# A fixed order for the prologue of a two-block transformer kernel: norm weight spread by a product, first weight chunk loaded ahead of the second token tile

## The chip, the core and the metric

The kernel runs on one core of a Trainium2 chip. The metric is the device time of one execution in microseconds (us). Before the change three runs gave 1746.03, 1747.23 and 1747.4 us; the median is 1747.23.

Engines in the profile: PE is TensorE's matmul, PEld its weight load, DVE is VectorE, ACT is ScalarE, POOL is GpSimd, and SP is SyncE, whose queue (SPq) issues every DMA of this kernel in order.

## The reference, cut to what matters

The input `x` has 256 tokens of width 1024. The first step is a norm and one wide projection; all that follows (dilated attention, retention, memory attention, a mixture of experts, and a second block of two layers) needs it.

```
def rms_norm(x, w, eps=1e-6):
    y = x * rsqrt(mean(x * x, axis=-1) + eps)
    return y * w

x = x + parallel_mixer(rms_norm(x, norm_mix_w), w_in, ...)   # proj = h @ w_in, cut into q, k, v, rq, rk, rv, rg
x = x + memory_cross_attention(...)
x = x + hierarchical_moe(...)        # 32 experts, 200 MB of weights
# second block: two layers of ffn, four mixers, ffn
```

Everything is float32. A dense product is made of three: each operand is split into a high part in the float32r type (`xh`, `wh`) and the low remainder (`xl`, `wl`), and high x high, high x low and low x high are added up in PSUM.

## The kernel before, in words

The tokens are two tiles of 128 (t = 0, 1). The width of 1024 is eight blocks of 128 (k = 0 to 7). A dense weight is packed in chunks of 1 MB; for a projection of 512 columns a chunk holds four k blocks, and `weight` (L265) cuts it into two parts of two k blocks. For each part ACT writes `wh` (L279, a copy with rounding) and DVE or POOL writes `wl` (L283, raw minus `wh`). The buffers `wh` and `wl` have three slots (`wsp`), so part n+3 can be converted only when the products of part n are done for both token tiles. The ring of raw chunks has four buffers.

Which engine writes `wl` is set by two lists: the first two parts of the kernel go to POOL (`on_pool = [None, None]`, L203), and of the others every fourth by a running count (`nw`, `pool_mod = 4`, L206, L282). From the second block's mixers on, `pool_mod` is 0.

`mixer1` (L522) is the prologue. It clears a tile, multiplies it with itself WARM = 18 times on PE (L531, work that nobody reads), loads `x` tile 0 in two halves, `ident`, `x` tile 1, the norm weight as a broadcast to 128 partitions (L238, 512 KB written), and the first weight chunk in two halves (L260). For each token tile ACT squares and sums (L1003), DVE and POOL form 1/rms (L416, L418: POOL's `pow`), DVE multiplies by it and by the norm weight (L508), PE transposes four blocks at a time (L401), ACT and DVE split the result into `xh` and `xl` (L391, L392). Then `dilated` (L569) projects K, Q and V by `dense_nat` (L314); K's, with `stagger=True`, is the first dense product of the kernel: 48 products of 128 x 512 in four parts.

Who goes first: the tile framework takes the instructions in program order as priority and arranges each engine's queue with a planner that models times; only where `manual_schedule` names an engine does the written order hold on it. An engine runs its queue strictly in order. So an instruction may stand in front of another that was written earlier. SPq, too, is arranged by the planner. `issue_after` ties one instruction behind another on the same engine.

`retention_start` (L608) opens the buffers of the retention, loads `ret_gn_w` as a broadcast (L238) and computes `log_decay` (L639), 23 small DVE instructions one after another with one exponential on ACT; its result is used by the retention, about 100 us later. It also clears four pieces of `rqp` on POOL (L558).

Much later the weights of the experts (`mraw`, L823) stream through buffers that the memory attention gives up one by one; L968 consumes them.

## Time and profile before

| | |
|---|---|
| Median of three runs | 1747.23 us |
| Profiled execution, its own device time | 1748.11 us |
| Its span in the trace | 1746.5 us |
| PE busy | 1582.8 us, 91% of the span |
| DVE, ACT, POOL busy | 48%, 38%, 16% |
| Chain that ended last | PE 54%, DMA 21%, DVE 3%, issue 2%, POOL 1%, ACT 1% |
| DMA | 419.07 MB, mean 240 GB/s |

The chain that ended last is followed back from the last instruction: at each step to what released it. A busy PE is not PE at its peak, since a product at the lower granted clock counts as busy as well. A wait for several semaphores is put down to the one that came last.

### The profile page before, as it was taken

How to read it: one execution, taken by the hardware profiler on the slowest of the kernel's cores; microseconds unless marked ns; L12 is line 12 of the kernel's file. 1: busy time of each engine (PE TensorE's matmuls, PEld its weight loads, DVE VectorE, ACT ScalarE, POOL GpSimd, SP SyncE). 2: the span in 40 equal slices, each digit the busy share in tenths (PEclk: the TensorE clock that was granted, in tenths of full speed). 3: DMA queues.
4: the chain of work that ended last, by engine and by line, in shares of the span. 5: the costliest groups of instructions: out<-in, count | busy, mean ns of one | idle time of the engine just before them, and what ended most of it. 6: DMA issues, size and time to landing. Idle time of an engine off the chain costs nothing.

```text
span 1746.5 us, 24953 instructions
## 1 busy us (share of the span) xinstructions
PE 1582.8 (91%) x10070; PEld 1217.7 (70%) x10070; DVE 839.2 (48%) x1468; ACT 657.5 (38%) x1125; POOL 286.5 (16%) x253
## 2 busy tenths in 40 slices
PE   8999898877767776899999989999999999989998
PEld 6777774322211221699988769999999988779997
DVE  5657653000000000454577675556655667765555
ACT  4655441000000000444445745444444536734442
POOL 4223321100000000222233250000100041340000
PEclk9999998888878777999999989999999999989999
DMA  8444859999999999855553235556455634155551
GB/s 273 143 178 158 319 192 421 417 421 421 420 420 421 421 420 421 346 180 186 196 180 126 96 145 181 185 190 241 145 194 181 247 110 141 49 185 187 178 190 73
DMA packets 66188, 419.07 MB, mean 240 GB/s; under 512 B 10642, under 2 KB 12178, under 8 KB 18706
## 3 DMA queue, kind: packets, MB, share of 16 engines
q1 hardware_dynamic: 66064, 417.39, 63.1%
q8 instruction: 82, 1.34, 0.3%
q14 instruction: 42, 0.33, 0.1%
HBM read 416.32 MB, written 1.05 MB: 239 GB/s over the span
## 4 chain that ended last, share of the span: by engine, by line
PE 54%; DMA 21%; DVE 3%; issue 2%; POOL 1%; ACT 1%; DVEq 0%; SPq 0%; POOLq 0%; ACTq 0%
DMA mraw<-in_wm 21%; PE ps L310 17%; PE ps L312 17%; PE ps L311 17%; PE ps L401 1%; PE ps L480 1%; DVE xa L1211 1%; PE ps L968 0%; PE ps L945 0%; POOL rq L418 0%; DVE wl L283 0%; DVE xl L392 0%; DVE lnst L1239 0%; POOL ropet L1423 0%; DMA raw<-in_wd 0%
## 5 line engine op out<-in xcount | busy, mean ns | idle before, releaser
L283 DVE TENSOR_TENSOR wl<-raw,wh 128x1024 fp32r<-128x1024 f32 (+2 forms) x314 | 389.5, 1251 | 300.8 <-ACT wh L279 298.2
L279 ACT ACTIVATE wh<-raw 128x1024 fp32r<-128x1024 f32 (+2 forms) x356 | 370.9, 1052 | 349.7 <-PE ps L311 179.9
L310 PE MATMUL ps<-xh,wh 128*128 128x256 f32 x1424 | 402.1, 282 | 3.4 <-ACT cv L1511 3.4
L312 PE MATMUL ps<-xh,wl 128*128 128x256 f32 x1424 | 401.4, 282 | 0.0
L311 PE MATMUL ps<-xl,wh 128*128 128x256 f32 x1424 | 401.0, 282 | 0.0
L310 PEld LDWEIGHTS ps<-xh,wh 128*128 128x128 f32 x1424 | 268.3, 188 | 6.6 <-ACT cv L1511 3.8
L311 PEld LDWEIGHTS ps<-xl,wh 128*128 128x128 f32 x1424 | 268.4, 188 | 1.4
L312 PEld LDWEIGHTS ps<-xh,wl 128*128 128x128 f32 x1424 | 268.4, 188 | 0.8
L968 PE MATMUL ps<-mraw,xg 128*32 128x512 f32 x1024 | 171.4, 774 | 69.1 <-DMA mraw<-in_wm 68.9
L312 PE MATMUL ps<-wh,xl 128*128 128x512 f32 (+3 forms) x520 | 190.0, 370 | 7.4 <-DVE xl L392 7.2
L310 PE MATMUL ps<-wh,xh 128*128 128x512 f32 (+3 forms) x520 | 190.3, 375 | 4.8 <-ACT xh L391 4.1
L311 PE MATMUL ps<-wl,xh 128*128 128x512 f32 (+3 forms) x520 | 191.6, 369 | 2.7 <-POOL wl L283 1.3
L968 PEld LDWEIGHTS ps<-mraw,xg 128*32 128x32 f32 x1024 | 26.5, 120 | 201.5 <-DMA mraw<-in_wm 166.1
L418 POOL TENSOR_TENSOR rq<-rv,mhalf 128x1 f32<-128x1 f32 (+4 forms) x46 | 46.9, 1020 | 729.0 <-DVE rv L416 726.3
L283 POOL TENSOR_TENSOR wl<-raw,wh 128x1024 fp32r<-128x1024 f32 x42 | 103.6, 2472 | 280.9 <-ACT wh L279 182.0
L974 DVE TENSOR_TENSOR mf<-ps,mf 128x512 f32<-128x512 f32 x8 | 5.5, 692 | 238.1 <-PE ps L968 234.1
L312 PEld LDWEIGHTS ps<-wh,xl 128*128 128x128 f32 x520 | 100.6, 194 | 24.0 <-DVE xl L392 11.2
L310 PEld LDWEIGHTS ps<-wh,xh 128*128 128x128 f32 x520 | 100.6, 194 | 22.7 <-ACT xh L391 7.5
L311 PEld LDWEIGHTS ps<-wl,xh 128*128 128x128 f32 x520 | 101.0, 194 | 18.4 <-POOL wl L283 3.4
L311 PE MATMUL ps<-wl,hf 128*128 128x512 f32 x256 | 100.1, 391 | 0.0
L312 PE MATMUL ps<-wh,hf 128*128 128x512 f32 x256 | 100.1, 391 | 0.0
L310 PE MATMUL ps<-wh,hf 128*128 128x512 f32 x256 | 98.2, 390 | 0.0
(355 smaller groups left out, 1980.1 us busy)
## 6 DMA issues: line engine op xcount, KB each, us to landing
mraw<-in_wm SPq DMA_DIRECT2D x191, 1024.0 KB, 19.8
raw<-in_wd SPq DMA_DIRECT2D x179, 1024.0 KB, 4.9
raw<-in_wd SPq DMA_DIRECT2D x8, 512.0 KB, 10.9
raw<-in_wd SPq DMA_DIRECT2D x4, 832.0 KB, 4.3
bc_ln_g<-in_ln_g SPq DMA_DIRECT2D x6, 512.0 KB, 5.8
bc_ln_b<-in_ln_b SPq DMA_DIRECT2D x6, 512.0 KB, 6.6
raw<-in_wd SPq DMA_DIRECT2D x4, 768.0 KB, 4.2
bias<-in_bias SPq DMA_DIRECT2D x4, 512.0 KB, 5.8
```

The source lines that it names most:

```text
L279: s.nc.scalar.activation(h[:, :n], rc, AF.Copy)
L283: i = eng.tensor_tensor(l[:, :n], rc, h[:, :n].bitcast(F32), op=OP.subtract)
L310: mm(out, lhsT=lh, rhs=rh, start=start, stop=False)
L311: mm(out, lhsT=lh, rhs=rl, start=False, stop=False)
L312: mm(out, lhsT=ll, rhs=rh, start=False, stop=stop)
L401: s.nc.tensor.transpose(ps[:, b * 128:b * 128 + 128], src[:, b * 128:b * 128 + 128], s.ident)
L418: s.last_pow = s.nc.gpsimd.tensor_tensor(q, r, s.mhalf[:, :n], op=OP.pow)
L480: s.nc.tensor.matmul(out, lhsT=v(j), rhs=pt[:, 2 * i + j], start=first and j == 0, stop=last and j == 1)
L968: nc.tensor.matmul(ps[32 * e:32 * e + 32], lhsT=xg[:, k, 32 * e:32 * e + 32], rhs=w[:, e * FF:e * FF + FF], start=k == 0, stop=k == NK - 1 ...
L974: nc.vector.tensor_tensor(f, gu[1], f, op=OP.mult)
L1211: nc.vector.scalar_tensor_tensor(z[:, cs], z[:, cs], mv[:, 0:1], g[:, cs], op0=OP.subtract, op1=OP.mult)
```

## The change

- `mixer1` calls a new function `norm1`. The norm weight is loaded as one row of 4 KB and put on all partitions by two PE products with a row of ones (K = 1, float32), into the two PSUM banks "b". DVE's multiplications read it there.
- WARM is 14 instead of 18; the two products stand behind the tenth.
- SPq's written order is: first half of `x` tile 0, the row, second half, `ident`, the first chunk in two halves, `x` tile 1.
- On PE, ACT and DVE the prologue has a written order: tile 0 through its norm, the first chunk's conversion (both `wl` on DVE), 12 products of tile 0 with the first chunk, then tile 1 through its norm.
- `on_pool` is empty and `nw` starts at -4; the first chunk's parts aren't counted. So the parts that go to POOL are, in the order of the parts, numbers 6, 10, 14, ... instead of 1, 2, 4, 8, 12, ...
- `retention_start` stands before the products and no longer loads `ret_gn_w` or computes `log_decay`; both come after `dilated`, and `log_decay`'s first DVE instruction is tied behind the last `wl` that DVE had been given until then.

```
-WARM = 18
+WARM = 14
-        s.on_pool = [None, None]
+        s.on_pool = []
-        s.nw, s.pool_mod = 0, 4
+        s.nw, s.pool_mod = -4, 4
     def dense_nat(s, x, n, done, stagger=False, first=None):
+        if first:
+            w[0] = first(ps[0])
         if stagger:
             for t in range(NT):
-                for c in range(2):
+                for c in range(1 if first and not t else 0, 2):
                     part(t, c)
     def mixer1(s):
...
-            wn = s.bcast(p, "norm_mix_w", D)
-            s.ahead = [s.raw(cuts=2)]
-            for t in range(NT):
-                for c, z in s.rms(p, x[t], wn):
-                    s.tsplit(hs, t, z[:, c * 512:], k0=4 * c, n=4)
-        o = s.xsplit()
...
+            with ExitStack() as c1:
+                first = s.norm1(s.pool(c1, "rms1", side="right"), x, hs)
+                r = s.retention_start(ctx)
+                o = s.xsplit()
+                with ExitStack() as c2:
+                    s.dilated(c2, hs, o, first)
+            r["gnw"] = s.bcast(r["p"], "ret_gn_w", 512)
+            r["lg"] = s.log_decay(r["p"])
+    def norm1(s, p, x, hs):
+        nc = s.nc
+        halves = [slice(c * 512, c * 512 + 512) for c in range(2)]
+        warm = p.tile([128, 512], F32R, name="warm")
+        nc.vector.memset(warm.bitcast(F32), 0.0)
+        one = p.tile([1, 128], F32, name="one")
+        nc.vector.memset(one, 1.0)
+        row = p.tile([1, D], F32, name="row")
+        for c, cs in enumerate(halves):
+            nc.sync.dma_start(x[0][:, cs], s.a["x"][:128, cs])
+            if not c:
+                nc.sync.dma_start(row, s.a["norm_mix_w"])
+        nc.sync.dma_start(s.ident, s.a["ident"])
+        raw = s.raw(cuts=2)
+        nc.sync.dma_start(x[1], s.a["x"][128:])
+        z = [p.tile([128, D], F32, name=f"z{t}") for t in range(NT)]
+        ps, wn = s.bank("mm"), [s.bank("b") for _ in range(2)]
+        w = [[s.wsp.tile([128, CH // 2], F32R, name=n, tag=n) for n in ("wh", "wl")] for _ in range(2)]
+        part = [raw[:, i * 1024:i * 1024 + 1024] for i in range(2)]
+        hi = lambda i: nc.scalar.activation(w[i][0], part[i], AF.Copy)
+        lo = lambda i: nc.vector.tensor_tensor(w[i][1], part[i], w[i][0].bitcast(F32), op=OP.subtract)
+        def tile(t, between):
+            q = s.rms_scale(z[t], x[t])
+            for c, cs in enumerate(halves):
+                nc.vector.scalar_tensor_tensor(z[t][:, cs], x[t][:, cs], q, wn[c], op0=OP.mult, op1=OP.mult)
+            tp = [s.transpose4(z[t][:, cs]).rearrange("p (b c) -> p b c", b=4) for cs in halves]
+            tk = slice(t * 128, t * 128 + 128)
+            between()
+            for c in range(2):
+                nc.scalar.activation(hs[0][:, 4 * c:4 * c + 4, tk], tp[c], AF.Copy)
+            for c in range(2):
+                h = hs[0][:, 4 * c:4 * c + 4, tk]
+                nc.vector.tensor_tensor(hs[1][:, 4 * c:4 * c + 4, tk], tp[c], h.bitcast(F32), op=OP.subtract)
+        order = s.tc.manual_schedule(engines={mybir.EngineType.PE, mybir.EngineType.Activation, mybir.EngineType.DVE})
+        def first(out):
+            with order:
+                for i in range(WARM):
+                    if i == WARM - 4:
+                        for c, cs in enumerate(halves):
+                            nc.tensor.matmul(wn[c], lhsT=one, rhs=row[:, cs], start=True, stop=True)
+                    nc.tensor.matmul(ps, lhsT=warm[:, :128], rhs=warm, start=True, stop=True)
+                tile(0, lambda: hi(0))
+                hi(1)
+                lo(0)
+                lo(1)
+                for a, b in ((0, 0), (1, 0), (0, 1)):
+                    for k in range(4):
+                        cs = slice(k % 2 * 512, k % 2 * 512 + 512)
+                        nc.tensor.matmul(out, lhsT=hs[a][:, k, :128], rhs=w[k // 2][b][:, cs], start=a + b + k == 0,
+                                         stop=False)
+                tile(1, lambda: None)
+            return w
+        return first
     def log_decay(s, p):
-        nc.vector.scalar_tensor_tensor(na, d, -1.0, d, op0=OP.mult, op1=OP.min)
+        s.issue_after(nc.vector.scalar_tensor_tensor(na, d, -1.0, d, op0=OP.mult, op1=OP.min), s.last_lo)
```

## Rows read from the trace of the kernel before

**Rows 1.** Stretches: length, busy PE PEld DVE ACT POOL, granted clock, DMA share, GB/s.
```profile
25.00:50.00 25.00, 24.31 (x112) 19.73 (x110) 19.50 (x48) 11.48 (x17) 9.85 (x8) 1.00 0.56 187
260.00:264.00 4.00, 4.00 (x19) 3.34 (x18) 1.38 (x2) 0.00 (x0) 0.00 (x0) 1.00 1.01 424
360.00:710.00 350.00, 252.49 (x1412) 61.72 (x1411) 22.52 (x54) 14.93 (x25) 17.76 (x23) 0.79 1.01 420
```

**Rows 2.** SP's timeline (start, length in us) and its waits (total, times, longest).
```profile
250.89 9.72 SPq L823 DMA_DIRECT2D mraw<-in_wm  x9
...
SPq L823 <- POOL wl L283: 13.0, 1, 13.0
```

**Rows 3.** PE's timeline of the prologue: start, length, instruction, idle before and releaser.
```profile
1.60 6.62 PE L531 MATMUL ps<-warm 128*128 128x512 f32 x18 [1.60 <-DVE warm L528]
11.11 1.32 PE L401 MATMUL ps<-ident,rms 128*128 128x128 f32 x8 [2.89 <-DVE rms L508]
...
15.32 0.80 PE L311 MATMUL ps<-wl,xh 128*128 128x512 f32 x1 [0.41 <-POOL wl L283]
16.33 0.63 PE L310 MATMUL ps<-wh,xh 128*128 128x512 f32 x1
16.76 0.63 PE L311 MATMUL ps<-wl,xh 128*128 128x512 f32 x1
20.84 0.39 PE L310 MATMUL ps<-wh,xh 128*128 128x512 f32 x1
21.07 0.40 PE L311 MATMUL ps<-wl,xh 128*128 128x512 f32 x1
```

**Rows 4.** Half-microsecond stretches of PE: length, busy, granted clock, DMA share, GB/s.
```profile
13.00:13.50 0.50, 0.43 (x1) 0.75 0.99 378
...
20.00:20.50 0.50, 0.50 (x3) 0.92 1.03 418
...
225.50:226.00 0.50, 0.00 (x0) 1.00 0.12 49
...
228.00:228.50 0.50, 0.50 (x4) 0.79 1.00 426
```

**Rows 5.** ACT's timeline of the prologue and the K projection.
```profile
8.50 0.63 ACT L1003 ACTIVATE rms<-x 128x512 f32<-128x512 f32 x1 [3.46 <-DMA x<-in_x]
11.47 1.06 ACT L279 ACTIVATE wh<-raw 128x1024 fp32r<-128x1024 f32 x1 [1.64 <-DMA raw<-in_wd]
12.43 0.58 ACT L391 ACTIVATE xh<-ps 128x512 fp32r<-128x512 f32 x1
21.10 1.06 ACT L279 ACTIVATE wh<-raw 128x1024 fp32r<-128x1024 f32 x1 [0.51 <-PE ps L312]
29.04 1.06 ACT L279 ACTIVATE wh<-raw 128x1024 fp32r<-128x1024 f32 x1 [0.58 <-PE ps L312]
```

**Rows 6.** DVE's timeline of the prologue, and one instruction of `log_decay`.
```profile
10.31 2.74 DVE L508 SCALAR_TENSOR_TENSOR rms<-x,rq,bc_norm_mix_w 128x512 f32<-128x512 f32 x4 [0.23 <-DMA bc_norm_mix_w<-in_norm_mix_w]
13.04 0.69 DVE L392 TENSOR_TENSOR xl<-ps,xh 128x512 fp32r<-128x512 f32 x1
30.13 1.23 DVE L283 TENSOR_TENSOR wl<-raw,wh 128x1024 fp32r<-128x1024 f32 x1 [0.73 <-ACT wh L279]
36.15 0.17 DVE L659 TENSOR_TENSOR lsacc<-lsacc,lsw 128x8 f32<-128x8 f32 x1
```

**Rows 7.** POOL's timeline of the prologue.
```profile
5.37 0.55 POOL L418 TENSOR_TENSOR rq<-rv,mhalf 128x1 f32<-128x1 f32 x1 [3.98 <-DVE rv L416]
12.60 4.99 POOL L283 TENSOR_TENSOR wl<-raw,wh 128x1024 fp32r<-128x1024 f32 x2 [1.89 <-ACT wh L279]
```

**Rows 8.** The chain that ended last: start, length, what.
```profile
463.94 3.60 PE ps L994 x4
```

**Rows 9.** PE's waits from 20 to 110 us: total, times, longest.
```profile
PE ps L311 <- POOL wl L283: 0.9, 1, 0.9
PE ps L401 <- DVE lsacc L661: 0.7, 1, 0.7
```

## The prediction

> **What bounds the kernel now.** I read the page's shares first, then the stretches, then the timelines of the first 30 us engine by engine. From 25 us on PE is busy 24.31 of 25 us at the full clock [rows 1]: behind the prologue the K, Q and V projections are one dense stream of products. The experts are bound by the DMA: from about 260 to 710 us it moves 420 GB/s at a share of 1.0 [rows 1]. That stream begins with nine loads that SP issues from 250.89 us [rows 2], into buffers which the memory attention frees as PE goes on. So an earlier start of PE's dense stream passes through to the end one for one, if nothing between reorders: what is to be sized is the start.

> In the prologue PE's warm-up ends at 8.22; it idles 2.89 us until DVE has multiplied by the broadcast norm weight (10.31, released by that weight's DMA), transposes, and waits at 15.32 for the first chunk's low part from POOL [rows 3, 6]. POOL needs 4.99 us for two such parts [rows 7], DVE 1.23 for one [rows 6]. The granted clock falls to half at about 13.25 and comes back at about 20.0 [rows 4]; meanwhile products start 0.43 us apart (16.33, 16.76), afterwards 0.23 (20.84, 21.07) [rows 3]. A slot of `wh` is free when both tiles have used it: the fourth part is converted at 21.10, the seventh, which needs the end of K's last part, at 29.04 [rows 5]. So **K's 48 products end at 29.0 us**; that is the mark which I recompute.

> **The change, part by part.** Landing times I take by position in SP's queue. Before, the third block of 512 KB (`x` tile 1) was there at 8.50, the next (the broadcast) at 10.31, the next (first half of the chunk) at 11.47 [rows 5, 6]. After, these places are taken by the chunk's halves and then `x` tile 1, with one more small load in front, whose issue I estimate at 0.4 us: first half 8.9, second 10.7, tile 1 11.9. If the broadcast was itself slow they come up to 1.5 us earlier; the chain below wins at most 0.5 by it, since ACT then does its steps in the same order.

> Warm-up: ten products 0.43 apart end at 1.60 + 4.4 = 6.0. The two float32 products of 512 columns I price by four of the same width that take 3.60 us, 0.9 each [rows 8]; theirs have 128 rows and these one, so each may cost from 0.23 (a product of one pass at full clock) to 1.8 (half clock). I take 0.9, the same type and width: 7.8, and four warm products at 0.23 end at 8.7. The four dropped ones cost nothing, as nobody reads them. 1/rms of tile 0 is ready at 5.37 + 0.55 [rows 7], plus 0.4 for the later second half: 6.3; the first product at 6.9 ends later. DVE multiplies (2.74/4 = 0.69 each [rows 6]) until 7.7 and 8.5; eight transposes take 1.32 [rows 3]: 8.7 to 10.0. Nothing waits on the price of the two products unless it passes about 1.2 each.

> ACT in the written order: first `wh` (1.06 [rows 5]) 8.9 to 10.0, two `xh` (0.58 each) to 11.2, second `wh` to 12.25. DVE: `xl` (0.69 [rows 6]) 10.6 to 11.3 and to 12.0, the two `wl` (1.23) to 13.25 and 14.5. PE: high x high for k0 and k1 at 10.6, the rest from 12.25, the last products with `wl` 14.5 to 15.0: twelve products done. Taking `wl` from POOL thus costs DVE 2.5 us which tile 1 waits for: its two small DVE steps stand behind (14.9), POOL's `pow` 0.55 (15.5), two multiplications (16.25, 16.95), transposes to 17.65, first `xh` at 17.6. Meanwhile only the third slot is free, so PE can do six products of tile 0 on k4 and k5, four of them surely. From 17.65 thirty products remain, 30 x 0.23 = 6.9: **K ends at 24.5, 4.5 us earlier.** Bounds: 24.0 if the chunk lands early; 25.1 if the planner puts the third `wl` on DVE into `pow`'s gap (0.6 later); 26.0 if ACT and DVE convert nothing of the second chunk before tile 1 is through (third `wh` at 18.25, its `wl` done at 20.55, twenty-four products after that). So 3.0 to 5.0.

> Next, the later stages. PE's waits between 20 and 110 us that this touches are 0.9 on a `wl` of POOL and 0.7 behind `log_decay` on DVE [rows 9]. The `wl` parts of POOL move from the second chunk of each projection to the first, and `log_decay` behind the last `wl` of V; so both waits may go (1.6 gained), or come back in another place: `log_decay` is 23 instructions of about 0.2 us from start to start (0.17 busy [rows 6]), 4.6 us of chain on DVE in the dilated attention. I take a gain of 0.5, the range is -4.6 to +1.6. The loads of `ret_gn_w` and of the decays leave SP's queue at 20 us; behind them stood raw chunks that have a ring of four ahead, so I cost that at nothing; without that cover it is about 0.4 each, three of them. Clearing `rqp` on POOL, four instructions, falls where POOL now has no `wl`: nothing. The banks "b" are free at 17, and Q needs them at 24.5: nothing; if not, Q's start would wait.

> Sum: 4.5 + 0.5 = 5.0 us. The profiled execution took 1748.11 around a span of 1746.5, 0.9 above the median 1747.23; the difference applies to either, so **1742.2 us** against the median.

> **Rivals.** *The clock falls again.* It fell at 13.25 after the idle 2.89 us and a run of transposes, and at about 228.2 after a shorter gap (PE idle from 225.5 to 226.0) and a few products [rows 3, 4]. After the change PE has transposes from 8.7, two products, a gap of 1.1 us, and a gap before tile 1. Against it: no gap is as long as the first. If it falls at 13 and stays low until 20, transposes end 0.7 later, four more products remain undone or run at 0.43 instead of 0.23, and K ends near 26.4: gain 2.6 + 0.5 = 3.1, **1744.1**. [...]

> *The moved chain costs what the prologue gives.* `log_decay`'s 4.6 us on DVE stand in front of the softmax: 4.5 - 4.6, about zero, **1747.3**. For it: PE already waited once behind that chain [rows 9]. Against: it is split over short instructions among which the planner puts others.

> *Slower: the experts' stream starts later.* Place: SP's queue before 250.89. SP once stood 13.0 us in front of an `mraw` load, held by a `wl` on POOL [rows 2]. The count that chooses POOL's parts is shifted, so the part that holds SP may now be one in front of the nine loads. If they wait 13.0 more, the stream, which has no slack until 710, ends 13.0 - 5.0 = 8.0 us later than before: **1755.2**. It decides from 5.0 us of wait on. Against: those loads also follow PE, which is early.

> *Chances.* A measurement tells 0.2%, 3.5 us, from no change. Forecast, with 1738 to 1743.7 as its own range (gains of 3.5 to 9, the larger if both later waits go and the planner's new order helps): 0.52. Clock: 0.20; moved chain and the closed order of the second chunk: 0.16, all within 0.2%. Later stream: 0.12. So faster 0.52, same 0.36, slower 0.12. The range 1736 to 1750 holds the first three with a later re-planning of a few us either way, and leaves out the late stream.

> **What would show it.** Right: the norm's multiplication at about 7.0 with PSUM as its operand; the first dense product near 10.6; twelve done by 15.0; tile 1's first `xh` near 17; the seventh `wh` conversion at 24.5 instead of 29.04; a clock of 1.0 from 6 us on; the nine `mraw` loads at about 246. Wrong: half clock between 13 and 20; `xh` of tile 1 after 18.5; PE waiting behind `lsacc` after 50 us; or the 420 GB/s stretch beginning no earlier than before although K ends early.

## The result, and the profile after

The changed kernel takes 1759.27 us (median of five runs, 1755.08 to 1761.74) against 1746.96 for the kernel before beside it: a ratio of 1.0068, 95% interval 1.0057 to 1.0079. It is **12 us slower**; 1742.2 was forecast, with 1736 to 1750 as the range. The profiled execution took 1757.29 us around a span of 1755.6, 9.2 more than the profiled one of before.

The stretches of [rows 1], after:

```profile
25.00:50.00 25.00, 24.23 (x102) 18.88 (x101) 14.83 (x21) 11.72 (x15) 10.78 (x6) 0.93 0.52 173
260.00:264.00 4.00, 4.00 (x20) 3.39 (x19) 2.43 (x6) 1.15 (x3) 0.00 (x0) 1.00 0.92 295
```

The clock has a dent in the dense stream (0.93 instead of 1.00), and at 260 us the experts' loads are not yet at full rate (295 GB/s instead of 424). The loads themselves, answering to [rows 2]:

```profile
14.81 0.43 SPq L694 DMA_DIRECT2D decay<-in_ret_decay_b  x1
...
197.65 2.48 SPq L872 DMA_DIRECT2D mraw<-in_wm  x5
253.90 10.12 SPq L872 DMA_DIRECT2D mraw<-in_wm  x7
```

The first `mraw` load leaves SP at 197.65; before it left at 191.51. So two thirds of the profiled loss arise before 200 us. The loads that [rows 2] show from 250.89 start at 253.90. PE's timeline of the prologue, answering to [rows 3]:

```profile
5.82 1.98 PE L593 MATMUL ps<-row,one 1*128 1x512 f32 x4
...
10.50 1.22 PE L602 MATMUL ps<-wh,xh 128*128 128x512 f32 x2
17.66 1.29 PE L406 MATMUL ps<-ident,z 128*128 128x128 f32 x8 [0.35 <-DVE z L577]
24.33 0.50 PE L314 MATMUL ps<-wh,xl 128*128 128x512 f32 x1 [1.61 <-DVE xl L585]
...
28.04 0.63 PE L312 MATMUL ps<-wh,xh 128*128 128x512 f32 x1
28.46 0.63 PE L313 MATMUL ps<-wl,xh 128*128 128x512 f32 x1
```

Down to the first dense product this is the forecast: the two row products in 1.98 us, the first dense product at 10.50 (forecast 10.6). Then PE stands 1.61 us for an `xl` of tile 1, and soon afterwards, from 25.65 to 28.9, products start 0.42 to 0.43 apart instead of 0.23, at a granted clock of 0.50 from 26 to 29. What held that `xl` is seen on DVE, whose columns are those of [rows 6]:

```profile
18.96 0.69 DVE L585 TENSOR_TENSOR xl<-ps,xh 128x512 fp32r<-128x512 f32 x1 [0.79 <-ACT xh L582]
23.51 0.17 DVE L712 TENSOR_SCALAR lg<-decay 128x8 f32<-128x8 f32 x1 [3.87 <-DMA decay<-in_ret_decay_b]
23.59 0.68 DVE L585 TENSOR_TENSOR xl<-ps,xh 128x512 fp32r<-128x512 f32 x1
```

Between the two `xl` the planner has put `lg`, a step of 8 columns of `log_decay` that needs only the decays (min(decay, 0)). The change ties only `na`, the chain's other first step, behind V. The decays' DMA, issued at 14.81, landed 8.6 us later, and DVE stood for it 3.87 us, with the second `xl` behind it, whose `xh` ACT had ended at 19.59. On ACT and POOL, answering to [rows 5, 7], the lambdas do the same:

```profile
24.44 0.21 ACT L1239 ACTIVATE ls<-ls 128x2 f32<-128x2 f32 x1 [4.86 <-DVE ls L1238]
24.55 2.94 ACT L279 ACTIVATE wh<-raw 128x1024 fp32r<-128x1024 f32 x3
...
30.69 1.06 ACT L279 ACTIVATE wh<-raw 128x1024 fp32r<-128x1024 f32 x1 [0.60 <-PE ps L314]
```

```profile
14.97 0.89 POOL L639 TENSOR_TENSOR qk<-col_attn_q_norm_w,col_attn_k_norm_w 128x1 f32<-128x1 f32 x1 [7.20 <-DMA col_attn_k_norm_w<-in_attn_k_norm_w]
16.15 0.58 POOL L423 TENSOR_TENSOR rq<-rv,mhalf 128x1 f32<-128x1 f32 x1
23.67 0.32 POOL L1236 TENSOR_TENSOR lm<-bc_diff_lambda 128x64 f32<-128x64 f32 x1 [6.95 <-DMA bc_diff_lambda<-in_diff_lambda]
```

ACT's exponential of the lambdas (`ls`) stands 4.86 us ahead of three `wh` conversions, so the fourth of K comes at 24.55 instead of 21.10, and the seventh, the mark of K's end, at 30.69. Before it was 29.04; the forecast was 24.5. POOL's `qk` holds tile 1's `pow` (`rq`) until 16.15, and `lm` has POOL stand for 6.95 us. Later PE waits, answering to [rows 9] (total, times, longest):

```profile
PE ps L312 <- DVE rqp L400: 2.3, 1, 2.3
PE ps L314 <- DVE xl L585: 1.6, 1, 1.6
```

The first of these ends at 64.33, and the granted clock is 0.50 from 64 to 70. One more wait lies far behind, at the start of the second block, behind a low part for which DVE needs 2.74 us, instead of about 1.2, beside one of POOL:

```profile
724.65 0.39 PE L313 MATMUL ps<-wl,xh 128*128 128x256 f32 x1 [2.30 <-DVE wl L283]
```

```profile
721.86 2.74 DVE L283 TENSOR_TENSOR wl<-raw,wh 128x1024 fp32r<-128x1024 f32 x1
...
721.15 2.36 POOL L283 TENSOR_TENSOR wl<-raw,wh 128x1024 fp32r<-128x1024 f32 x1 [77.78 <-DVE x L966]
```

### The profile page after: what moved, and what is told of

Read it like the earlier page. It is cut to its first block, busy times and chain, and to the rows that moved or that the text cites. A ratio compares the mean times of both kernels' runs of the same rounds, so it can differ in the third digit from the quotient of the medians.

```text
span 1755.6 us, 24956 instructions
## 1 busy us (share of the span) xinstructions
PE 1591.8 (91%) x10070; PEld 1221.3 (70%) x10070; DVE 840.9 (48%) x1471; ACT 659.0 (38%) x1125; POOL 281.6 (16%) x251
## 4 chain that ended last, share of the span: by engine, by line
PE 65%; DMA 24%; DVE 5%; issue 2%; POOL 2%; ACT 1%; SPq 0%; DVEq 0%; ACTq 0%; POOLq 0%
DMA mraw<-in_wm 23%; PE ps L312 20%; PE ps L314 19%; PE ps L313 19%; PE ps L406 2%; PE ps L485 2%; PE ps L1017 1%; DVE xa L1260 1%; POOL rq L423 1%; DVE wl L283 1%; PE ps L994 1%; DMA col_attn_q_norm_w<-in_attn_q_norm_w 1%; DMA decay<-in_ret_decay_b 0%; ACT wh L279 0%; DVE dtmp L757 0%
## 5 line engine op out<-in xcount | busy, mean ns | idle before, releaser
L283 DVE TENSOR_TENSOR wl<-raw,wh 128x1024 fp32r<-128x1024 f32 (+2 forms) x313 | 383.2, 1234 | 296.9 <-ACT wh L279 295.8
L1017 PE MATMUL ps<-mraw,xg 128*32 128x512 f32 x1024 | 175.4, 789 | 67.4 <-DMA mraw<-in_wm 67.2
L283 POOL TENSOR_TENSOR wl<-raw,wh 128x1024 fp32r<-128x1024 f32 x41 | 99.9, 2441 | 338.7 <-ACT wh L279 229.2
```

What stands on the lines that cost most here:

```text
L283: i = eng.tensor_tensor(l[:, :n], rc, h[:, :n].bitcast(F32), op=OP.subtract)
L1017: nc.tensor.matmul(ps[32 * e:32 * e + 32], lhsT=xg[:, k, 32 * e:32 * e + 32], rhs=w[:, e * FF:e * FF + FF], start=k == 0, stop=k == NK - 1 ...
```

## The experiments

Two theories stood at first. **A**: small steps with late operands, in front of tile 1's work on in-order engines, cost most of the 12 us. **D**: the shifted count, by which GpSimd gets other low parts, costs most of it. The table has every run's result. The ratio is to the kernel before, measured beside it; it is not the quotient of the two medians, so the two can differ. The marks are from one profiled execution of each kernel: the seventh `wh` conversion (K's end), the first product with `pt` and `va` (dilated attention), the first `mraw` load, and the span less that load (all that comes later).

| kernel | median us | ratio [95%] | 7th wh | first pt,va | first mraw | rest |
|---|---|---|---|---|---|---|
| before | 1747.0 to 1747.7 | | 29.04 | 74.20 | 191.51 | 1555.0 |
| changed | 1759.27 | 1.0068 [1.0057, 1.0079] | 30.69 | 80.11 | 197.65 | 1558.0 |
| before_pool_count | 1758.93 | 1.0063 [1.0049, 1.0077] | 28.87 | 83.47 | 201.34 | 1558.0 |
| before_chain_moved | 1747.80 | 1.0004 [0.9994, 1.0013] | 28.62 | 74.03 | 191.16 | 1554.7 |
| tie_small_steps | 1754.18 | 1.0039 [1.0026, 1.0053] | 26.68 | 75.05 | 194.41 | 1558.1 |
| pool_count | 1750.38 | 1.0017 [1.0008, 1.0026] | 30.61 | 77.11 | 194.56 | 1555.0 |
| both_and_late_chain | 1754.70 | 1.0045 [1.0031, 1.0058] | 29.87 | 74.70 | 195.89 | 1554.7 |
| ties_and_count | 1753.37 | 1.0026 [1.0015, 1.0036] | 33.09 | 79.90 | 197.35 | 1555.5 |
| chain_as_before | 1754.45 | 1.0040 [1.0026, 1.0053] | 32.39 | 81.19 | 198.13 | 1554.7 |
| chain_after_ret_proj | 1753.45 | 1.0037 [1.0023, 1.0050] | 29.99 | 73.78 | 193.76 | 1554.9 |
| pool_ties | 1746.02 | 0.9992 [0.9983, 1.0001] | 29.75 | 74.91 | 193.44 | 1554.2 |
| k_parts_on_dve | 1743.80 | 0.9991 [0.9981, 1.0001] | 26.08 | 69.90 | 188.31 | 1550.4 |
| full_row_product | 1744.55 | 0.9984 [0.9975, 0.9993] | 27.45 | 71.29 | 190.94 | 1555.0 |
| chain_at_q | 1746.35 | 0.9995 [0.9986, 1.0004] | 26.34 | 72.33 | 190.72 | 1553.6 |
| v_part_on_dve | 1748.31 | 1.0003 [0.9994, 1.0012] | 25.19 | 74.75 | 188.61 | 1553.4 |
| v_part_and_chain_at_q | 1746.40 | 0.9997 [0.9988, 1.0006] | 25.94 | 75.58 | 189.52 | 1553.7 |

The profiled execution is not always near its kernel's median: that of k_parts_on_dve took 1740.40 us (its other ten 1743.27 to 1749.15), that of v_part_on_dve 1743.68, of full_row_product 1747.55 and of pool_ties 1749.27. Differences of a microsecond or two between the marks of two kernels mean little.

**before_pool_count**: the kernel before, with the shift of the count alone.

```
-        s.nw, s.pool_mod = 0, 4
+        s.nw, s.pool_mod = -2, 4
```

> The kernel before with only the count that picks GpSimd's low parts shifted, to where the changed kernel has it from the second chunk on; the first two parts stay on GpSimd. Theory A: the prologue stays (seventh wh at about 29.0, as the first chunk's parts are where they were); the wait on GpSimd's low part in the projections goes or moves (within 1 us); FFN 0 starts 1.5 to 2.7 us later; together 1 to 3 us slower than before (ratio 1.0005 to 1.002). Rival D: the shift costs most of the loss by itself, 8 to 12 us (ratio 1.005 to 1.007).

Measured +11.5 us. Theory D holds, against what I expected: the shift alone costs as much as the whole change. One stretch of the kernel before, and then those of this run (columns as in [rows 1]):

```profile
60.00:62.00 2.00, 2.00 (x20) 2.00 (x18) 0.71 (x2) 0.73 (x2) 2.00 (x1) 1.00 0.00 0
```

```profile
60.00:62.00 2.00, 1.35 (x7) 0.70 (x7) 1.62 (x6) 1.97 (x5) 0.40 (x1) 1.00 0.79 311
62.00:64.00 2.00, 1.53 (x8) 1.10 (x8) 2.00 (x5) 0.90 (x3) 0.00 (x0) 0.88 0.39 164
64.00:66.00 2.00, 2.00 (x10) 1.35 (x9) 0.51 (x2) 0.00 (x0) 0.00 (x0) 0.50 0.00 0
...
72.00:74.00 2.00, 0.83 (x7) 0.63 (x6) 1.24 (x7) 1.44 (x7) 0.99 (x1) 0.94 0.71 211
74.00:76.00 2.00, 2.00 (x8) 1.68 (x8) 1.50 (x8) 1.44 (x6) 0.00 (x0) 0.50 0.77 252
```

Its PE and DVE around it:

```profile
61.82 0.66 PE L401 MATMUL ps<-ident,qn 128*128 128x128 f32 x4 [0.44 <-DVE qn L564]
62.95 0.50 PE L311 MATMUL ps<-wl,xh 128*128 128x512 f32 x1 [0.47 <-DVE wl L283]
...
73.66 0.52 PE L310 MATMUL ps<-kt,qt 64*128 64x256 f32 x1 [1.17 <-DVE mn L442]
```

```profile
57.38 1.23 DVE L283 TENSOR_TENSOR wl<-raw,wh 128x1024 fp32r<-128x1024 f32 x1 [0.28 <-ACT wh L279]
58.52 0.17 DVE L416 TENSOR_SCALAR rv<-hss 128x8 f32<-128x8 f32 x1
...
61.08 0.69 DVE L564 TENSOR_TENSOR qn<-ps,rq 128x512 f32<-128x512 f32 x1
61.68 1.21 DVE L283 TENSOR_TENSOR wl<-raw,wh 128x1024 fp32r<-128x1024 f32 x1
```

The kernel before has POOL write the sixteenth low part, at 59.65; DVE is busy only 0.71 of the 2 us from 60 on. With the shift that part falls to DVE, at 57.38, and `rv`, a step of q's norm whose input was there at 57.1, stands behind it for 1.4 us. `qn`, which needs `rv`, comes at 61.08 instead of 57.34, and the seventeenth part (61.68), which DVE writes in both kernels, stands behind `qn` and two softmax steps. PE waits 0.44 and 0.47 us for these two, and later 1.17 for a softmax step (`mn`). How the rest of the delay arises in the newly planned queues is not shown. PE works 1.35, 1.53 and later 0.83 of 2 us with no wait over 1.2, and after these thin stretches the clock is 0.50 for some 6 us each (64 to 70, 74 to 80). First `pt,va` is 9.3 later; by an estimate from these stretches, 12 us at half the clock, about 6 of them are low clock. The remaining 3.0 are in the last column: 1558 in every kernel with the shifted count (changed, before_pool_count, tie_small_steps), 1550 to 1556 in all others; it is the wait of 2.30 us at the second block's start with its low clock. Where the count is as before, that wait is about 0.8.

**tie_small_steps** and **pool_count**: the changed kernel with three DVE steps tied behind the last low part (`lg`, and in the same way `trir`, L854, and the lambdas' sum `ls`, L1238), and with the count put back.

```
-        nc.vector.tensor_scalar(lg, d, 0.0, None, op0=OP.min)
+        s.issue_after(nc.vector.tensor_scalar(lg, d, 0.0, None, op0=OP.min), s.last_lo)
...
```
```
-        s.nw, s.pool_mod = -4, 4
+        s.nw, s.pool_mod = -2, 4
```

> The changed kernel with three small DVE steps (min(decay,0), the lambda reduction, the cast of the triangle constant) held in DVE's queue behind the last low part of V; nothing else differs. Theory A (the prologue's end is lost because steps that wait for small, late loads stand in the in-order queues of DVE and ACT ahead of token tile 1): tile 1's two xl come adjacent near 19 to 20 us, the fourth wh conversion near 19 to 21 instead of 24.55, the clock stays at 1.00, the seventh wh conversion comes at about 25 instead of 30.69. That is about 5.5 us; the wait behind the log_decay chain near 64 us and the late low part at FFN 0 stay, so the time falls by about 5.5 from the changed kernel's, to 3 to 5 us above before (ratio about 1.002 to 1.003). Rival B (the fixed order itself ends the prologue late: DVE's low parts and tile 1's steps in line): the seventh conversion stays at 29 to 31 and the time within 2 us of the changed kernel. Rival C (the clock falls after the gap before tile 1 anyway): xl early, but a granted clock of 0.5 from about 20 to 28 and the seventh conversion at 27 to 28.

> The changed kernel with the count that picks GpSimd's low parts set two on, so that from the second chunk on GpSimd has the same parts as before. Theory A: the prologue's mark (seventh wh at 30.7) and the wait near 64 us stay; at FFN 0 PE's wait for the low part goes back from 2.30 to about 0.8 us and the clock does not fall there, so that step gives about 2.7 us: the time is about 2.7 below the changed kernel's, still 6 to 9 above before. Rival D (the shifted count is most of the loss): at least 8 us come back and the time is within 0.2% of before.

Ties: −5.1 us, K's mark 26.68; theory A holds for the prologue and theory B falls. Count: −8.9 us, more than the 2.7 expected, the mark unmoved. Each cures its own place.

**both_and_late_chain, ties_and_count, chain_as_before, chain_after_ret_proj**: ties and count together, with `log_decay` after retention_proj (lambdas too), where the change has it, after Q's projection (the edit below), and after retention_proj.

```
         s.dense_nat(hs, 512, qdone)
+        r["gnw"] = s.bcast(r["p"], "ret_gn_w", 512)
+        r["lg"] = s.log_decay(r["p"])
```

> The changed kernel with the three ties, with GpSimd's parts as before, and with ret_gn_w's load, log_decay and the lambdas called after retention_proj's products instead of after the dilated attention. Theory A: seventh wh near 25 us; no wait of PE behind DVE between 60 and 70; first product with pt and va near 68 to 70 instead of 80.1 (74.2 before); FFN 0 waits 0.8; the experts' stream starts 4 to 6 us before that of the kernel before, and the time is 1741 to 1744, about 0.998 of before. Rival E (what the prologue gives never reaches the end, because something between, the stretch 70 to 250, is paced by another engine): the prologue mark at 25 but the first mraw issue of the nine within 1 us of 250.9 and the time within 0.1% of before. Rival B: the mark stays at 29 to 31, the time 1747 to 1750.

> The changed kernel with the three ties and with GpSimd's parts as before; log_decay and ret_gn_w stay after the dilated attention. If the losses add up (prologue's small steps 5 of the 12 us, GpSimd's parts 9): the seventh wh conversion at 25 to 27 us as with the ties alone, the wait of 2.5 us behind the rqp step near 60 gone, one wait of 2 to 2.5 us behind lsacc or qn near 50 left: 1745 to 1747, ratio 0.999 to 1.000. Rival (the two are the same loss, a fall of the clock that one cure already takes away): no better than the better of the two, 1750.

> As the kernel with ties and count, and log_decay (with ret_gn_w's load) called after Q's projection, tied to Q's last low part, so that its 23 steps stand in DVE's queue where the kernel before had them. Theory: the later stages are then those of before, and the prologue's gain passes to the end: seventh wh at 25 to 26.7 against 29.04, first product with pt and va at 70.5 to 72 against 74.2, the nine mraw loads at 247 to 248.5, time 1742.5 to 1745 (ratio 0.9975 to 0.999). Rival (nothing of the prologue's gain gets through the dense stream, or later waits come back): 1747, ratio within 0.0005 of 1.

> As the kernel with ties and count, and log_decay called after retention_proj's products; the lambdas stay after the dilated attention. Theory: nothing of the chain between 40 and 70 us, so no wait over 1 us there and the first product with pt and va at 70.5 to 72; the chain comes near 104 to 116 us, in front of the memory norm's xl, and costs a wait of 2 to 2.8 us at about 115: 1744.5 to 1747. Rival (DVE has room there): equal to the kernel with the chain as before, within 1 us.

All four missed: 1753 to 1755, and K's mark back at 30 to 33. The two gains did not add up. POOL and PE of ties_and_count:

```profile
23.49 1.30 POOL L1236 TENSOR_TENSOR lm<-bc_diff_lambda 128x64 f32<-128x64 f32 x1 [6.76 <-DMA bc_diff_lambda<-in_diff_lambda]
24.75 1.74 POOL L848 TENSOR_TENSOR wr<-wr 128x288 f32<-128x288 f32 x1
26.46 2.33 POOL L283 TENSOR_TENSOR wl<-raw,wh 128x1024 fp32r<-128x1024 f32 x1
...
28.84 0.50 PE L313 MATMUL ps<-wl,xh 128*128 128x512 f32 x1 [4.33 <-POOL wl L283]
```

The count as before gives K's fourth low part to POOL. There `lm`, which stands for the lambdas' load, and the router's weights (`wr`) are in front of it, and PE waits 4.33 us; chain_as_before waits 3.95 and chain_after_ret_proj 2.60 there. It is theory A on the third engine. In both_and_late_chain this wait did not occur; its prologue was late because the row products ran at half speed (below), and it had 2.83 us of wait at 117 behind `xl`, after log_decay; chain_after_ret_proj had 2.62 in the same place.

**before_chain_moved**: the kernel before, with `log_decay` and `ret_gn_w` called after the dilated attention and `na` tied, as the change has it.

> The kernel before with one part of the change alone: ret_gn_w's load and log_decay called after the dilated attention, tied to the last low part of V on DVE; prologue and GpSimd's parts stay. Theory (a chain of 23 short DVE steps at V's end makes PE wait): the wait of 0.69 us behind lsacc at 44 goes, one of about 2.4 us comes near 51 to 56, with a low granted clock for some us behind it: 2 to 5 us slower, ratio 1.001 to 1.003. Rival (DVE has room there): within 1 us of before.

The wait came as expected (2.45 us behind `lsacc` at 51.46), but no low clock behind it, and the time is equal. So moving the chain costs nothing by itself in the kernel before; putting it back in the changed kernel (chain_as_before) gained nothing either.

**pool_ties**: ties_and_count, with `lm` (the first line below) and `wr` behind POOL's last low part. **k_parts_on_dve**: with, besides, K's fourth low part on DVE and `qk` behind K's `pow` (the other lines).

```
+            s.issue_after(nc.gpsimd.tensor_tensor(lm, lp[:, :, 0], lp[:, :, 1], op=OP.mult), s.pool_lo)
...
+        s.nw, s.pool_mod = -4, 4
...
         s.dense_nat(hs, 512, kdone, stagger=True, first=first)
+        s.nw = 4
+        s.issue_after(nc.gpsimd.tensor_tensor(qk, qw, kw, op=OP.mult), s.last_pow)
```

> The kernel with ties and count, and on GpSimd's queue two steps more held behind the last low part there: the product of the lambdas (lm) and the one of the router's weights (wr). In the run with ties and count lm started at 23.49, released by the lambdas' DMA, wr at 24.75, and K's fourth low part only at 26.46, for which PE stood 4.33 us. Theory G (a small step that waits for a late load stands in front of what PE needs, on GpSimd too): that part starts at 22 to 23, PE's wait in K falls from 4.33 to at most 1 us and the low clock at 30 to 33 goes; the fourth conversion stays at 21.0 and K's successor marks come 4 to 6 us earlier; time 1747 to 1749.5, 4 to 6 below that kernel's 1753.4. Rival (GpSimd is late by its own length, 2.3 to 3.3 us for one part): the wait stays over 2.5 us and the time within 2 us of 1753.

> The kernel with GpSimd's ties, and K's fourth low part on DVE (from Q on GpSimd has the parts of before); the product of the q and k norm weights, which waited for its DMA until 15.0 in front of tile 1's pow, is held behind K's pow. Theory G: tile 1's pow at about 15 instead of 16.15, tile 1's transposes 1 us earlier than 17.66, no wait of PE over 1 us in K, seventh wh at 25 to 26.7; from there the later stages of before, so the first product with pt and va at 70.5 to 72.5 and the time 1743 to 1746. Rival (the later stages lose it again by the planner's other order): K's mark as said, but the nine mraw loads not before 250 and the time 1747 or more.

pool_ties: −7.4 us against ties_and_count by the medians, 5.9 by the ratios; the fourth part of K starts as its `wh` is there (24.62, released by ACT), and PE's wait is gone. k_parts_on_dve: a median of 1743.80, but a ratio whose interval reaches 1.0001; in its profiled execution K's mark is 26.08 and `pt,va` 4.3 earlier than before. What is left there is a wait of 2.45 at 48.73. Its POOL, DVE and PE:

```profile
44.81 3.15 POOL L283 TENSOR_TENSOR wl<-raw,wh 128x1024 fp32r<-128x1024 f32 x1
...
45.66 2.33 DVE L710 TENSOR_SCALAR lsacc<-lsacc 128x8 f32<-128x8 f32 x1
...
48.73 0.63 PE L406 MATMUL ps<-ident,qn 128*128 128x128 f32 x4 [2.45 <-DVE lsacc L709]
```

A step of 8 columns takes 2.33 us instead of 0.17 and ends as POOL's part does. The trace of the kernel before has such a step too, which the prediction did not use: `lsw` at 32.90 took 2.37 us beside POOL's part.

**full_row_product**: k_parts_on_dve, with the weight's row under 127 rows of zeros, so that the two products use all rows. Besides, `one` has 128 rows, the row's load stands behind the second half of `x` tile 0, and DVE's first low part of `weight` is tied behind tile 1's `rv`.

```
-        row = p.tile([1, D], F32, name="row")
+        row = p.tile([128, D], F32, name="row")
+        nc.gpsimd.memset(row, 0.0)
```

> As the kernel with K's parts on DVE, but the two float32 products of the norm weight use all 128 rows: 127 rows of zeros under the weight (cleared on GpSimd at the start, 1.1 us), and a full 128 x 128 of ones; the row's DMA is issued after tile 0's second half. Theory H (behind products of one row the clock falls as behind an idle PE): in the other kernels with the row products the granted clock was 0.5 from 8.6 to 9.6 us on until 12 to 16; with 128 rows it stays at 1.00 until 16, the transposes of tile 0 take 1.0 to 1.1 us instead of 1.3 to 1.9, and K ends up to 1.5 us earlier; time 0 to 2 us below. Rival (the clock falls because of the gaps between transposes and the first dense products): the clock falls at 9 as before, times equal within 1 us.

The same microsecond of PE in k_parts_on_dve, and then in full_row_product (columns as in [rows 1]):

```profile
9.00:10.00 1.00, 1.00 (x6) 1.00 (x5) 0.25 (x1) 0.64 (x2) 0.00 (x0) 0.50 1.07 442
```

```profile
9.00:10.00 1.00, 0.75 (x8) 0.51 (x5) 0.10 (x1) 0.73 (x2) 0.00 (x0) 1.00 1.00 414
```

The low clock at 9 is gone, tile 0's transposes take 1.04 us, and the first dense product comes at 9.92 instead of 10.49; but in this execution the clock falls at 16 to 19, behind two thin microseconds (PE busy 0.57 and 0.24), and K ends later, not earlier (27.45). In the three kernels below, which have the same rows, it does not fall there, and K ends at 25.19 to 26.34, about where k_parts_on_dve has it. So no gain at K's end is shown. The time is equal to that of k_parts_on_dve; against before it is the one clear gain, 0.16%.

**chain_at_q, v_part_on_dve, v_part_and_chain_at_q**: full_row_product with `log_decay` after Q; with V's last low part on DVE (`and s.nw != 12` in the choice of the engine); with both.

> As the kernel with the full row product, and log_decay (with ret_gn_w's load) called after Q's projection and tied to Q's last low part on DVE, where the kernel before has its chain. Theory: the wait of 2.45 us behind lsacc at 50 (with a low clock until 55) goes, one of 0.7 us near 40 comes as in the kernel before; first product with pt and va at 68 to 69.5 instead of 71.29, time 1741 to 1743. Rival (the chain of 23 steps costs the same wherever it stands in the projections, since the DVE has no spare time there): within 1 us of 1744.5.

> As the kernel with the full row product (log_decay at V's end), and V's last low part, the twelfth, on DVE instead of GpSimd. In the run with K's parts on DVE, GpSimd wrote that part from 44.81 for 3.15 us, and beside it a step of 128 x 8 on DVE (lsacc) took 2.33 us instead of 0.17; PE then waited 2.45 us behind it and the clock was low until 53. Theory J (a low part on GpSimd holds DVE's next step as long as it runs): no DVE step of 128 x 8 over 0.5 us between 40 and 60, PE's longest wait there at most 1 us, time 1740 to 1743. Rival (DVE has no room: 1.2 us more of it are late instead): the wait stays over 1.5 us, now behind wl on DVE, time 1743.5 to 1746.

> The same with log_decay called after Q's projection, where the wait was 3.50 us behind qn at 51.14 and the time 1746.35. Theory J: the wait falls to at most 1 us and the time to 1741 to 1744. Rival: the wait stays over 1.5 us and the time over 1744.5.

chain_at_q missed: a wait of 3.50 behind `qn` in place of 2.45 behind `lsacc`. With the part off POOL no wait over 1 us is left between 45 and 55 at either place of log_decay, so POOL's part, not the chain, made it; in chain_at_q it was a whole low part on DVE that took 3.38 us beside it (47.01). One slow step of log_decay is left in v_part_on_dve, 1.86 us at 52.59 beside POOL's next part. But a wait behind `wl` on DVE comes at 58 (1.96 and 0.98), as the rival said, and `pt,va` is later. Neither time is better, and v_part_on_dve's median is 3.8 us worse, more than the rival's range. Theory J had the cause of the old wait right, and both its forecasts of the time missed.

## Why the prediction was wrong

By the marks, the profiled loss of 9.1 us is made up of 1.65 at K's end, 4.3 from there to the first `pt,va`, 0.2 to the first `mraw` load and 3.0 behind it. Forecast were a gain of 4.5 at K's end and 0.5 behind it; both terms failed.

- **Start to twelve products: right, in part by luck.** The norm's multiplication began at 7.80 (forecast 6.9), the row products ended at 7.80 (7.8), the first dense product began at 10.50 (10.6), tile 1's transposes ended at 18.95 (17.65): 1.3 late, as `rq` stood behind `qk` on POOL for a DMA. The price of 0.9 for a row product was luck. The four records of [rows 8] are two products, not four (the kernel's 32 products at L994 left 64 records), and they ran at a granted clock of 0.50 (the line below the list, of the kernel before); the two row products left four records as well, 1.98 us in all, but at a recorded clock of 1.00. The two errors cancel.
- **K ends at 24.5: failed.** The step costed tile 1 with nothing else in the queues. After it reads 30.69. Five small steps with late loads (`lg` and `ls` on DVE, `ls` on ACT, `qk` and `lm` on POOL) stood there. Tied back, with K's parts on DVE, the mark reads 25.2 to 27.5: a gain of 1.6 to 3.9 where 4.5 was forecast.
- **"The loads of `ret_gn_w` and of the decays leave SP's queue at 20 us ... I cost that at nothing": failed in its other half.** They left at 13.5 to 14.8, and with the steps tied back PE waits for no load; what waits for them did cost, and I took the tie on `na` as a tie on `log_decay`.
- **Later stages +0.5, range -4.6 to +1.6: the step that decided.** It asked which waits the shift of the count takes away (0.9 and 0.7 of [rows 9]) and not what DVE's queue holds up once it writes POOL's parts. The profiled run lost 7.4 there. Alone, in the kernel before, the shift cost 11.5: 9.8 before the first `mraw` load (9.3 of them before `pt,va`) and 3.0 at the second block's start in its profiled run. The latter place I had not examined; at the former most of it is low clock, not wait.
- **Moved chain as a rival (−4.6):** in the kernel before it costs nothing by itself.
- **Clock as a rival:** it did fall at 9 to 12, to 0.50, and what cost more was that it fell to 0.50 again at 25.6 to 28.9, at 64 to 70 and at 726 to 729.
- **The slower rival (1755.2)** had the cause right, the shifted count, and the sign. The place was wrong: PE at 60 to 80 us, not SP's queue at 250. There SP's waits for POOL's parts in front of `mraw` loads fell, from 13.0 us to 8.1. That its time is near the measured one is luck. The chance of slower was 0.12.
- **The gain that is left.** With every step tied back and the count as before from Q on, 2.8 us of the forecast 5.0 reach the end in full_row_product by its ratio. For k_parts_on_dve the medians differ by 3.7 us, but its ratio says 1.6 and is not clear of noise.

```profile
464.00:465.00 1.00, 1.00 (x2) 0.48 (x3) 0.00 (x0) 0.00 (x0) 0.00 (x0) 0.50 1.01 418
```

Open: the runs of k_parts_on_dve, but for the profiled one, lie in two groups, near 1743.6 and 1749.1, and those of v_part_on_dve are spread as widely (1743.68 to 1749.03); the runs do not show why. Nor was each of the five steps tied back alone, or the prologue's written order run without the rest of the change.

## What to carry to other kernels

Tie back every step that reads a moved load, not only the first one of its chain: in the changed kernel DVE stood 3.87 us for `lg`, ACT 4.86 for `ls` and POOL 6.95 for `lm`, steps of 0.17 to 0.32 us; behind the first two stood operands of PE, and in ties_and_count PE waited 4.33 us for a low part that stood behind `lm`. A counter that says which engine takes which part is a schedule for the whole kernel; before shifting it, read in each stage what stands behind the part on its new engine. Read PE's thin stretches with the clock that follows, not only its waits: in before_pool_count waits of 0.4 to 1.2 us were followed by some 6 us at a granted clock of 0.50, twice. It need not come so: before_chain_moved waited 2.45 us and chain_after_ret_proj 2.62 (at 116) with the clock at 1.00 behind it, and the runs do not show what makes the difference.
